# FFN way down by seven half-size products in three of four parts, and hidden columns mixed as they are made

## The chip, the cores and the metric

One core of one Trainium2 chip runs the whole program: two layers of a decoder trunk for one sequence of 512 tokens, 1024 wide, all in float32. The metric is the time of one execution on the device in microseconds (us). The engines are PE (TensorE, matrix products), DVE (VectorE), ACT (ScalarE), POOL (GpSimd) and SP (SyncE, which issues most of the loads).

## The reference, cut to what matters

Each layer is an FFN, a mix of attention and pooling, and a second FFN; so there are four FFNs, of 1024 by 2816.

```
def swiglu(h, w_gate, w_up, w_down):
    return (jax.nn.silu(h @ w_gate) * (h @ w_up)) @ w_down
...
for l in range(DEPTH):
    h = rms_norm(x, ffn1_norm[l])
    x = x + 0.5 * swiglu(h, ffn1_w_gate[l], ffn1_w_up[l], ffn1_w_down[l])
    ...
    h = rms_norm(x, ffn2_norm[l])
    x = x + 0.5 * swiglu(h, ffn2_w_gate[l], ffn2_w_up[l], ffn2_w_down[l])
return rms_norm(x, final_norm)
```

## The kernel before, in words

x is kept transposed in SBUF: eight blocks of 128 channels, each with 512 columns (the tokens). Every factor of a product is split into a rounded hi part and a lo part that holds the rest, and `mm3` (L95 to L97) makes each product of three matmuls: hi by hi, hi by lo, lo by hi.

The 2816 hidden channels of an FFN are 22 blocks of 128, taken as 11 pairs. For a pair, `plain` makes gate and up the direct way, with matmuls of 128x512 (one pair in each FFN, two in the first one); for the others, `mixed` makes them by Winograd's form of Strassen's method. Gate and up are there the two block rows of a matrix and the two halves of the tokens the two block columns, so that seven products take the place of eight. Each of them is 24 matmuls of 128x256 and needs mixed operands (the b's, made by `operands` at the start of an FFN) and mixed weights. Products are numbered by their operand, and are made in the order 1, 2, 6, 5, 7, 3, 4, in three PSUM banks (`ps_a`, `ps_g`, `ps_c`); some results are copied out by ACT (p1, w, p5 in `copied`, L451) and added by DVE. The pair's hidden columns, silu(gate) times up, are split by `hidden` into hhi and hlo.

The FFN runs in three parts, `PARTS`, of 4, 4 and 3 pairs. Behind each part's gate and up comes its way down: for each of the eight output blocks n, `down` makes 2 x nq products of 128x512 (three matmuls each) in a bank `ps_dn` and takes half of the sum off x (L499; the sign is turned in the hidden columns).

Weights come through two rings. `load_raw` has SP load blocks of up to 128x1024 into one of six raw buffers (wraw). `load_next` then makes the hi and lo part in one of five buffers each (whi, wlo). Most blocks are split by ACT and DVE (`split`, L143 and L144). A block by DMA goes another way: ACT writes the negative rounded value into wlo (L164), POOL issues a DMA that adds the block from HBM to it (L165, 512 KB each), and ACT casts the hi part (L166). For a mixed pair, `pair` plans seven blocks: products 1, 2 and 4 take theirs from memory as they are, by such a DMA; those of products 6, 5, 7 and 3 are sums of the four raw blocks, made on DVE (L175 to L178) and split there. `weights` hands out the next block and prepares the ones to come.

The order on each engine is the framework's scheduler's; a stretch marked `high_priority` may be moved ahead of others. Each engine then works through its own queue in order.

Of the kernel before, what the change touches and what calls it, by code (L numbers as in the profile page):

```python
# [11 lines left out]
F32 = mybir.dt.float32  # L12
# [9 lines left out]
L = 2  # L22
# [9 lines left out]
PARTS = ((0, 4), (4, 4), (8, 3))  # L32
# [38 lines left out]
def trunk(ctx: ExitStack, tc: tile.TileContext, xT, gu1, dn1, win_qk, win_v, win_u, poolw, wout, gu2, dn2, small, lams, consts, outT):  # L71
# [4 lines left out]
    act = ctx.enter_context(tc.tile_pool(name="act", bufs=25))  # L76
    tmp = ctx.enter_context(tc.tile_pool(name="tmp", bufs=8))
# [75 lines left out]
    def load_next(i):  # L153
# [15 lines left out]
        else:  # L169
            if step[0] == "sums":  # L170
                r = step[1] - 3
                load_raw(r + 3 + AHEAD_RAW)
                a11, a12, a21, a22 = raw_tiles[r : r + 4]
                u1 = wpool.tile([P, WSLOT], F32, name="wsum", bufs=1)
# [8 lines left out]
            split(hi, lo, raw)  # L183
# [22 lines left out]
    cst = cpool.tile([P, K_MASK], F32, name="cst")  # L206
# [130 lines left out]
    def triples(out, w, b, jj, start, stop, more):  # L337

        for i in range(4):
            c = slice((jj * 4 + i) * P, (jj * 4 + i + 1) * P)  # L340
            mm3(out, w[0][:, c], w[1][:, c], b[0][:, i, :], b[1][:, i, :], start and i == 0, stop and i == 3, more)

    def operands(norm, r):
# [13 lines left out]
        def parts(t):  # L357
            hi, lo = quarter("bhi", F32R), quarter("blo", F32R)
            split(hi, lo, t)
            return hi, lo  # L360
# [23 lines left out]
    def ffn(norm, l, nxt, first=None):  # L384
        st = {}
        hh, hl = [], []

        def hidden(u):

            hi, lo = arena("hhi"), arena("hlo")  # L390
            split(hi, lo, u)
            hh.append(hi)
            hl.append(lo)

        def plain(first, at):

            banks = [bank("ps_pl") for _ in range(4)]
            gates, u = [], pair32("u")
# [30 lines left out]
            for jj in range(2):  # L429
                v = u[:, jj, :]  # L430
                nc.vector.scalar_tensor_tensor(v, banks[2 + jj], -1.0, st["r"], ALU.mult, ALU.mult)
                nc.vector.tensor_mul(v, v, gates[jj])
            hidden(u)

        def halves(t):
            return t.rearrange("p (j s) -> p j s", j=2)

        def mixed():

            b = st["b"]  # L440
            u = pair32("u")

            def product(q, ps, start):
                w = weights()
                for jj in range(2):
                    triples(ps[:, jj * HS : (jj + 1) * HS], w, b[q], jj, start and jj == 0, True, True)

            def copied(ps, name):
                t = single(name)
                with tc.high_priority(PRIO):  # L450
                    nc.scalar.copy(t, ps)  # L451
                return t

            a, g, c = bank("ps_a"), bank("ps_g"), bank("ps_c")
            product(1, a, True)
            p1 = copied(a, "p1")
            product(2, g, True)
# [4 lines left out]
            product(6, a, False)  # L462
            w = copied(a, "w")
            product(5, c, True)
            p5 = copied(c, "p5")
            product(7, a, False)
            up2 = single("up2")
            with tc.high_priority(PRIO):
                nc.vector.tensor_add(up2, a, p5)
            product(3, c, False)  # L470
# [4 lines left out]
            product(4, a, False)  # L475
            with tc.high_priority(PRIO):
                nc.vector.tensor_mul(u[:, :, :HS], halves(a), halves(g1))
            nc.vector.tensor_mul(u[:, :, HS:], halves(up2), halves(g2))
            hidden(u)

        for hf, (q0, nq) in enumerate(PARTS):
            hh.clear()
            hl.clear()
            for q in range(q0, q0 + nq):
                if q >= plain_pairs(first):
                    mixed()
                elif q:
                    plain(None, -2)
# [12 lines left out]
            tail = hf == len(PARTS) - 1  # L501
            last = tail and isinstance(nxt, Final)
            if first and hf == 0:
                constants()
            for n in range(KD - 2 if last else KD):
                down(bank("ps_dn"), n, weights())
                if tail:
                    nxt.add(n)
# [17 lines left out]
    def mix(norm, l, nxt):  # L526
        st = {}

        def qk_project(h):
# [12 lines left out]
            if h == 0:  # L542
# [5 lines left out]
                st["cos"], st["sin"] = single("cosr"), single("sinr")  # L548
                nc.gpsimd.tensor_mul(st["cos"], cst[:, K_COS : K_COS + S], r)
                nc.gpsimd.tensor_mul(st["sin"], cst[:, K_SIN : K_SIN + S], r)  # L550
# [120 lines left out]
        def u_project(pair):  # L671
            dh, dl = arena("dhi"), arena("dlo")

            def done(i, ps):
# [15 lines left out]
                nc.vector.tensor_mul(e[:, :w], cur[:, :w], cst[:, K_CNT : K_CNT + w])  # L690
# [99 lines left out]
    def first_project(ps):  # L790
# [4 lines left out]
        for b in (A11, A12):  # L795
            raw.append(wpool.tile([P, 2, 4, P], F32, tag="wraw", name="wraw", bufs=6))
# [20 lines left out]
    def constants():  # L817
        nc.sync.dma_start(lam, lams)
        nc.sync.dma_start(cst, consts[:, :K_MASK])
# [120 lines left out]
```

## Time and profile before

| | us |
|---|---|
| median of 3 runs (1766.63 to 1768.07) | 1768.03 |
| the profiled execution | 1764.0 |
| its span | 1762.2 |
| PE busy (98% of the span) | 1728.4 |
| PE weight loads busy (89%) | 1565.5 |
| DVE busy (65%) | 1137.4 |
| ACT busy (54%) | 946.4 |
| POOL busy (12%) | 208.7 |

The span goes from the first to the last instruction; the execution's own time has 1.8 us more around it. Busy times overlap, since the engines run beside one another. A matmul's duration in a row is longer than its share of PE's time, because matmuls are pipelined: the time of one is read from how many start in a stretch. The granted clock, 0.995 in the mean, is the share of full speed that TensorE was given.

### The profile page before, as it was taken

The page shows a single profiled execution, that of the slowest core. Times are in us where ns is not written, and L with a number is a line of the kernel's source. Part 1 is how long each engine was busy: PE and PEld are TensorE (multiplying, and loading weights), DVE is VectorE, ACT ScalarE, POOL GpSimd, SP SyncE. Part 2 cuts the span into 40 slices and gives each one's busy share as a digit, 9 for nine tenths or more (in the row PEclk, how much of TensorE's full clock was granted, in tenths as well). Part 3 has the DMA queues.
Part 4 walks back from the last instruction along what each step waited for, and adds up shares of the span by engine and source line. Part 5 has one row for each costly group of instructions (what it writes and reads, how often), then busy time and mean ns, then how long its engine had stood idle before and what let it go on. Part 6 is the DMA issues. An engine that isn't in the chain of part 4 may idle for free.

```text
span 1762.2 us, 26872 instructions
## 1 busy us (share of the span) xinstructions
PE 1728.4 (98%) x10936; PEld 1565.5 (89%) x10936; DVE 1137.4 (65%) x1507; ACT 946.4 (54%) x1294; POOL 208.7 (12%) x215
## 2 busy tenths in 40 slices
PE   9899999999999999999999999999999999999997
PEld 7889989888788989989889899898887889899996
DVE  6845646577968746646587465466789596466463
ACT  7635626555566626526556265364555665364463
POOL 1000001120022001001210010012100400010001
PEclk9999999999999999999999999999999999999998
DMA  9455746422235737737657376374122647375551
GB/s 285 121 155 147 190 116 158 143 86 75 72 92 134 197 106 168 192 87 169 181 124 195 84 182 185 96 169 147 42 86 68 151 105 201 95 185 165 118 146 48
DMA packets 71723, 240.66 MB, mean 137 GB/s; under 512 B 7856, under 2 KB 12592, under 8 KB 71600
## 3 DMA queue, kind: packets, MB, share of 16 engines
q1 hardware_dynamic: 52304, 169.18, 30.3%
q0 software_dynamic: 19152, 69.74, 21.9%
q8 instruction: 85, 1.39, 0.3%
q14 instruction: 38, 0.31, 0.0%
q10 hardware_dynamic: 144, 0.03, 0.0%
HBM read 236.82 MB, written 2.10 MB: 136 GB/s over the span
## 4 chain that ended last, share of the span: by engine, by line
PE 87%; DVE 4%; DMA 4%; issue 2%; ACT 2%; SPq 0%; POOL 0%; POOLq 0%; DVEq 0%; ACTq 0%
PE ps_dn L96 9%; PE ps_dn L95 9%; PE ps_dn L97 9%; PE ps_a L97 8%; PE ps_a L96 8%; PE ps_a L95 8%; PE ps_c L95 4%; PE ps_c L96 4%; PE ps_c L97 4%; DMA wlo<-gu 3%; PE ps_g L97 2%; PE ps_g L95 2%; PE ps_g L96 2%; PE ps_pl L97 2%; PE ps_pl L95 2%
## 5 line engine op out<-in xcount | busy, mean ns | idle before, releaser
L143 ACT CAST whi<-wraw 128x1024 fp32r<-128x1024 f32 (+2 forms) x275 | 273.7, 997 | 417.1 <-PE ps_dn L96 146.3
L144 DVE TENSOR_TENSOR wlo<-wraw,whi 128x1024 fp32r<-128x1024 f32 (+2 forms) x275 | 317.6, 1157 | 109.3 <-ACT whi L143 107.6
L97 PE MATMUL ps_a<-bhi,wlo 128*128 128x256 f32 x1248 | 354.7, 284 | 4.9 <-DMA wlo<-gu 4.9
L95 PE MATMUL ps_a<-bhi,whi 128*128 128x256 f32 x1248 | 354.6, 284 | 0.8 <-ACT whi L166 0.5
L96 PE MATMUL ps_a<-blo,whi 128*128 128x256 f32 x1248 | 354.6, 284 | 0.0
L96 PE MATMUL ps_dn<-hlo,whi 128*128 128x512 f32 (+1 forms) x716 | 276.6, 386 | 0.0
L97 PE MATMUL ps_dn<-hhi,wlo 128*128 128x512 f32 (+1 forms) x716 | 276.0, 386 | 0.0
L95 PE MATMUL ps_dn<-hhi,whi 128*128 128x512 f32 (+1 forms) x716 | 275.7, 386 | 0.0
L165 POOL DMA_DIRECT2D wlo<-gu x133 | 116.3, 877 | 1117.7 <-ACT wlo L164 846.3
L97 PEld LDWEIGHTS ps_a<-bhi,wlo 128*128 128x128 f32 x1248 | 240.7, 193 | 5.6 <-DMA wlo<-gu 5.6
L95 PEld LDWEIGHTS ps_a<-bhi,whi 128*128 128x128 f32 x1248 | 240.6, 193 | 1.9 <-ACT whi L166 0.7
L96 PEld LDWEIGHTS ps_a<-blo,whi 128*128 128x128 f32 x1248 | 240.7, 193 | 0.8
L166 ACT CAST whi<-wraw 128x1024 fp32r<-128x1024 f32 x133 | 139.3, 1049 | 135.2 <-PE ps_dn L96 62.2
L499 DVE SCALAR_TENSOR_TENSOR x<-ps_dn,x 128x512 f32<-128x512 f32 (+1 forms) x98 | 66.6, 680 | 192.2 <-PE ps_dn L97 192.2
L95 PE MATMUL ps_c<-bhi,whi 128*128 128x256 f32 x624 | 177.0, 284 | 5.7 <-ACT bhi L143 5.7
L96 PE MATMUL ps_c<-blo,whi 128*128 128x256 f32 x624 | 176.8, 283 | 0.0
L97 PE MATMUL ps_c<-bhi,wlo 128*128 128x256 f32 x624 | 176.7, 283 | 0.0
L96 PEld LDWEIGHTS ps_dn<-hlo,whi 128*128 128x128 f32 x716 | 134.5, 188 | 28.0 <-DVE hlo L144 1.4
L97 PEld LDWEIGHTS ps_dn<-hhi,wlo 128*128 128x128 f32 x716 | 134.5, 188 | 26.9
L95 PEld LDWEIGHTS ps_dn<-hhi,whi 128*128 128x128 f32 x716 | 134.5, 188 | 26.7
L164 ACT ACTIVATE wlo<-wraw 128x1024 fp32r<-128x1024 f32 x133 | 140.3, 1057 | 0.2 <-DMA wraw<-gu 0.2
L95 PEld LDWEIGHTS ps_c<-bhi,whi 128*128 128x128 f32 x624 | 119.9, 192 | 6.3 <-ACT bhi L143 6.3
(171 smaller groups left out, 3231.8 us busy)
## 6 DMA issues: line engine op xcount, KB each, us to landing
wraw<-gu SPq DMA_DIRECT2D x174, 512.0 KB, 3.7
wlo<-gu POOLq DMA_DIRECT2D x133, 512.0 KB, 7.1
wraw<-dn SPq DMA_DIRECT2D x64, 512.0 KB, 4.5
wraw<-dn SPq DMA_DIRECT2D x32, 384.0 KB, 3.1
wraw<-wqk SPq DMA_DIRECT2D x16, 512.0 KB, 3.5
wraw<-wo SPq DMA_DIRECT2D x16, 512.0 KB, 3.6
wraw<-wv SPq DMA_DIRECT2D x8, 512.0 KB, 3.5
wraw<-wu SPq DMA_DIRECT2D x8, 512.0 KB, 3.6
```

The source lines that it names most:

```text
L95: nc.tensor.matmul(out, a_hi, b_hi, start=start, stop=False, skip_group_check=more)
L96: nc.tensor.matmul(out, a_hi, b_lo, start=False, stop=False, skip_group_check=more)
L97: nc.tensor.matmul(out, a_lo, b_hi, start=False, stop=stop, skip_group_check=more)
L143: nc.scalar.copy(hi, raw)
L144: nc.vector.tensor_sub(lo, raw, hi.bitcast(F32))
L164: nc.scalar.mul(lo[:, :n], raw[:, :n], -1.0)
L165: nc.gpsimd.dma_start(lo[:, :n], src, accum_op=ALU.add)
L166: nc.scalar.copy(hi[:, :n], raw[:, :n])
L499: nc.vector.scalar_tensor_tensor(x[:, n, ts], ps[:, ts], -0.5, x[:, n, ts], ALU.mult, ALU.add)
```

## The change

The way down of three parts is now made by seven half-size products as well. `PARTS` becomes 3, 3, 3 and 2 pairs; only the last part keeps `down`. For a part of nq pairs, `mixed_down` makes the eight output blocks as two halves (n = 0, 1) of four; in each half the two pairs of output blocks, the two blocks of each hidden pair and the two halves of the tokens are the blocks of the method. A product there is 6 x nq = 18 matmuls of 128x256, in the banks `ps_da`, `ps_dg` and `ps_dc`, and two to four updates of x on DVE (L531, L534) belong to it in place of one per output block. In the first half, products 1 and 2 are written so that what needs the newest hidden pair comes behind what doesn't.

`hidden` also makes the four mixed columns that these products need (ehi, elo, L432 to L438). A plain pair's last steps (up by gate, and `hidden`) are put off: they are a `finish` that the next mixed pair calls behind its fourth product. The down weights of these parts are planned by `pair`, three of seven blocks by DMA (384 KB each). The ring of raw weights has five buffers in place of six, the two pools act and tmp one more each. The table of cosines and sines is loaded for each mix instead of kept.

```
-PARTS = ((0, 4), (4, 4), (8, 3))
+PARTS = ((0, 3), (3, 3), (6, 3), (9, 2))
...
-                for n in range(KD):
-                    block(dn[hf][l, n])
+                if hf < len(PARTS) - 1:
+                    for n in range(2):
+                        pair(dn[hf][l, n])
+                else:
+                    for n in range(KD):
+                        block(dn[hf][l, n])
...
-            raw = wpool.tile([P, WSLOT], F32, name="wraw", bufs=6)
+            raw = wpool.tile([P, WSLOT], F32, name="wraw", bufs=5)
...
+        def hidden(first, second):
             hi, lo = arena("hhi"), arena("hlo")
-            split(hi, lo, u)
+            hs, ls = slots(hi), slots(lo)
+            if st["mixed"]:
+                split(hs[:, 3, :], ls[:, 3, :], second[:, 1, :])
+            else:
+                split(hs[:, 1::2, :], ls[:, 1::2, :], second)
+            split(hs[:, 0::2, :], ls[:, 0::2, :], first)
...
+            nc.vector.tensor_sub(e5, first[:, 0, :], second[:, 0, :])
+            nc.vector.tensor_sub(e7, second[:, 1, :], second[:, 0, :])
+            split(es[:, 0:2, :], fs[:, 0:2, :], halves(e))
...
+            nc.vector.scalar_tensor_tensor(e6, e5, -1.0, second[:, 1, :], ALU.mult, ALU.subtract)
+            nc.vector.scalar_tensor_tensor(e4, e6, -1.0, first[:, 1, :], ALU.mult, ALU.subtract)
+            split(es[:, 2:4, :], fs[:, 2:4, :], halves(e))
...
             p5 = copied(c, "p5")
+            if "finish" in st:
+                st.pop("finish")()
...
+        def mixed_down(n, nq):
...
+            if n == 0:
+                w1, w2 = weights(), weights()
+                product(a, w1, b[1], True, False, range(nq - 1))
+                product(g, w2, b[2], True, False, range(nq - 1))
+                product(a, w1, b[1], False, True, range(nq - 1, nq))
+                p1 = copied(a, "p1", -0.5)
+                product(g, w2, b[2], False, True, range(nq - 1, nq))
+            else:
+                product(a, weights(), b[1], True)
+                p1 = copied(a, "p1", -0.5)
+                product(g, weights(), b[2], True)
+            add(x1[:, :, first], g, -0.5)
+            plus(x1[:, :, first], p1)
+            product(a, weights(), b[6], False)
+            w = copied(a, "w", -0.5)
+            product(c, weights(), b[5], True)
+            p5 = copied(c, "p5", 0.5)
+            product(a, weights(), b[7], False)
+            with tc.high_priority(PRIO):
+                add(x2[:, :, second], a, 0.5)
+            plus(x2[:, :, second], p5)
+            product(c, weights(), b[3], False)
+            add(x1[:, :, second], c, -0.5)
+            plus(x1[:, :, second], w)
+            product(a, weights(), b[4], False)
+            add(x2[:, :, first], a, 0.5)
...
-            for n in range(KD):
-                down(bank("ps_dn"), n, weights())
+            if not tail:
+                for n in range(2):
+                    mixed_down(n, nq)
+                continue
```

What moves on the engines is seen at three places. The first is ACT's queue in the first FFN's way down. Before, at its first part, the queue holds casts of whole blocks behind the last hidden columns:

```order
L143 CAST whi<-wraw 128x1024
L143 CAST hhi<-u 128x1024
L143 CAST whi<-wraw 128x1024 x3
L166 CAST whi<-wraw 128x1024
L164 ACTIVATE wlo<-wraw 128x1024
L166 CAST whi<-wraw 128x1024
L164 ACTIVATE wlo<-wraw 128x1024
L143 CAST whi<-wraw 128x1024
```

After, at its second part, from product 1's copy in the first half on (blocks of 128x768 are the way down's, p and w the copies out of PSUM, L358):

```order
L358 ACTIVATE p_2044<-ps_da 128x512
L147 CAST ehi<-e_1998 128x512
L168 ACTIVATE wlo<-wraw 128x768
L170 CAST whi<-wraw 128x768 x2
L358 ACTIVATE w<-ps_da 128x512
L358 ACTIVATE p_2104<-ps_dc 128x512
L168 ACTIVATE wlo<-wraw 128x768 x2
```

And in the second half of the same part:

```order
L358 ACTIVATE p_2214<-ps_da 128x512
L170 CAST whi<-wraw 128x768
L168 ACTIVATE wlo<-wraw 128x768
L170 CAST whi<-wraw 128x1024
L358 ACTIVATE w<-ps_da 128x512
L168 ACTIVATE wlo<-wraw 128x1024
```

The negative copies (L168) for the second half's first two products now stand behind the copies of the third and fourth product (w and p_2104); those of the next gate and up pair (128x1024) stand in the second half in the same way.

The second place is POOL's queue in the same FFN. Before, its DMAs are all for gate and up:

```order
L165 DMA wlo<-gu 128x1024 x2
L298 TENSOR_TENSOR rT<-ms,nhalf 128x4
L165 DMA wlo<-gu 128x1024 x29
L251 TENSOR_TENSOR ssum<-ssum,sq 128x512 x7
```

After:

```order
L169 DMA wlo<-gu 128x1024 x2
L304 TENSOR_TENSOR rT<-ms,nhalf 128x4
L169 DMA wlo<-gu 128x1024 x5
L169 DMA wlo<-dn 128x768 x6
L169 DMA wlo<-gu 128x1024 x9
L169 DMA wlo<-dn 128x768 x6
L169 DMA wlo<-gu 128x1024 x9
L169 DMA wlo<-dn 128x768 x6
L169 DMA wlo<-gu 128x1024 x6
L257 TENSOR_TENSOR ssum<-ssum,sq 128x512 x7
```

Six DMAs for down weights now stand between those for gate and up, three times in each FFN.

The third place is PE's queue in the first mixed pair of the second FFN, at the end of its sixth product. Before (bhi_5366 is the operand of product 4):

```order
L96 MATMUL ps_c_5399<-blo_5363,whi_5430 128x256
L97 MATMUL ps_c_5399<-bhi_5362,wlo_5431 128x256
L95 MATMUL ps_a_5397<-bhi_5366,whi_5461 128x256
L96 MATMUL ps_a_5397<-blo_5367,whi_5461 128x256
L97 MATMUL ps_a_5397<-bhi_5366,wlo_5462 128x256
```

After (bhi_6007 is the operand of product 1, and ps_a_6351 the next pair's bank):

```order
L96 MATMUL ps_c_6076<-blo_6049,whi_6107 128x256
L97 MATMUL ps_c_6076<-bhi_6048,wlo_6108 128x256
L95 MATMUL ps_a_6351<-bhi_6007,whi_6169 128x256
L96 MATMUL ps_a_6351<-blo_6008,whi_6169 128x256
L97 MATMUL ps_a_6351<-bhi_6007,wlo_6170 128x256
```

The next pair's first product stands here ahead of this pair's last, product 4.

## Rows read from the trace of the kernel before

**Rows 1.** The page: busy time of each engine, shares of the chain of waits.

```profile
PE 1728.4 (98%) x10936; PEld 1565.5 (89%) x10936; DVE 1137.4 (65%) x1507; ACT 946.4 (54%) x1294; POOL 208.7 (12%) x215
...
PE 87%; DVE 4%; DMA 4%; issue 2%; ACT 2%; SPq 0%; POOL 0%; POOLq 0%; DVEq 0%; ACTq 0%
```

**Rows 2.** Windows by stage, first FFN: first gate/up stretch, way down, second gate/up stretch.

```profile
core 0: us, PE busy (x) PEld busy (x) DVE busy (x) ACT busy (x) POOL busy (x), PEclk, DMA share, GB/s
53.00:100.00 47.00, 42.49 (x337) 41.90 (x336) 34.98 (x40) 27.52 (x33) 3.50 (x4) 0.96 0.61 164
100.00:143.56 43.56, 43.56 (x194) 36.07 (x193) 18.91 (x21) 11.29 (x11) 1.75 (x2) 1.00 0.40 102
143.56:224.19 80.63, 80.63 (x673) 80.63 (x672) 52.39 (x53) 52.10 (x61) 8.75 (x10) 1.00 0.71 183
```

**Rows 3.** PE's waits over the span: total us, times, longest.

```profile
PE ps_c L95 <- ACT bhi L143: 5.7, 3, 1.9
...
PE ps_a L97 <- DMA wlo<-gu: 4.9, 3, 4.0
```

**Rows 4.** Timelines of PE, ACT and POOL, 192.3 to 204.4: start us, duration us.

```profile
192.39 0.28 PE L97 MATMUL ps_a<-bhi,wlo 128*128 128x256 f32 x1
...
192.64 1.05 ACT L166 CAST whi<-wraw 128x1024 fp32r<-128x1024 f32 x1 [0.19 <-PE ps_a L96]
193.59 0.58 ACT L451 COPY w<-ps_a 128x512 f32<-128x512 f32 x1
194.07 1.06 ACT L164 ACTIVATE wlo<-wraw 128x1024 fp32r<-128x1024 f32 x1
...
195.42 0.88 POOL L165 DMA_DIRECT2D wlo<-gu  x1 [2.49 <-ACT wlo L164]
...
204.27 0.28 PE L97 MATMUL ps_a<-bhi,wlo 128*128 128x256 f32 x1
```

**Rows 5.** Landings, stretches 100:143, 143:213, 275:285; then those issued 155.10, 175.26, 195.42.

```profile
DMA to landing us min/median/max: 5.3/5.4/5.6
...
DMA to landing us min/median/max: 5.8/7.0/7.6
...
DMA to landing us min/median/max: 7.9/8.2/8.2
...
DMA to landing us min/median/max: 6.8/6.8/6.8
...
DMA to landing us min/median/max: 6.2/6.2/6.2
...
DMA to landing us min/median/max: 7.1/7.1/7.1
```

**Rows 6.** Groups of instructions, shapes apart, whole span: busy us, mean ns, idle before.

```profile
L144 DVE TENSOR_TENSOR wlo<-wraw,whi 128x1024 fp32r<-128x1024 f32 x231 | 281.9, 1223 | 89.0 <-ACT whi L143 88.3
...
L143 ACT CAST whi<-wraw 128x768 fp32r<-128x768 f32 x32 | 26.7, 836 | 52.4 <-issue 23.4 <-PE ps_dn L96 13.6 <-PE ps_c L96 8.2
```

**Rows 7.** The page's DMA issues: count, size, median us from issue to landing.

```profile
wraw<-dn SPq DMA_DIRECT2D x64, 512.0 KB, 4.5
wraw<-dn SPq DMA_DIRECT2D x32, 384.0 KB, 3.1
```

**Rows 8.** Second FFN, first mixed pairs: timeline of POOL and PE, landing of that DMA.

```profile
569.52 0.86 POOL L165 DMA_DIRECT2D wlo<-gu  x1 [2.66 <-PE ps_c L97]
...
DMA to landing us min/median/max: 7.0/7.0/7.0
...
575.24 0.28 PE L97 MATMUL ps_a<-bhi,wlo 128*128 128x256 f32 x1
```

**Rows 9.** Windows behind the starts of three FFNs (columns as in rows 2).

```profile
66.00:88.00 22.00, 18.04 (x138) 17.83 (x137) 15.21 (x16) 13.25 (x16) 2.62 (x3) 0.92 0.75 187
...
562.00:584.00 22.00, 20.68 (x171) 20.57 (x171) 21.79 (x24) 17.68 (x22) 2.57 (x3) 1.00 0.62 142
...
1422.00:1444.00 22.00, 20.11 (x152) 19.70 (x151) 20.40 (x24) 15.75 (x18) 2.60 (x3) 0.92 0.55 130
```

More of the change, by code (lines that the diff above doesn't have):

```diff
@@ L172, in load_next @@
                 load_raw(r + 3 + AHEAD_RAW)
-                a11, a12, a21, a22 = raw_tiles[r : r + 4]
-                u1 = wpool.tile([P, WSLOT], F32, name="wsum", bufs=1)
+                n = raws[r].shape[-1]
+                a11, a12, a21, a22 = (raw[:, :n] for raw in raw_tiles[r : r + 4])
+                u1 = wpool.tile([P, WSLOT], F32, name="wsum", bufs=1)[:, :n]
                 nc.vector.tensor_add(u1, a21, a22)
@@ L182, in load_next @@
                 raw = sums[step[2]][step[1]]
-            split(hi, lo, raw)
+            n = raw.shape[-1]
+            split(hi[:, :n], lo[:, :n], raw)
         loaded.append((hi, lo))
@@ L335, in run, with product, copied, halves @@
             pass
[L337 to L341, printed above, removed]
+    def product(ps, w, b, start, stop=True, ks=None):
+        ks = ks or range(len(b))
+        for jj in range(2):
+            out = ps[:, jj * HS : (jj + 1) * HS]
+            for i in ks:
+                c = slice((jj * len(b) + i) * P, (jj * len(b) + i + 1) * P)
+                mm3(out, w[0][:, c], w[1][:, c], *b[i], start and jj == 0 and i == ks[0], stop and i == ks[-1], True)
+    def copied(ps, name, scale=None):
+        t = single(name)
+        with tc.high_priority(PRIO):
+            if scale is None:
+                nc.scalar.copy(t, ps)
+            else:
+                nc.scalar.mul(t, ps, scale)
+        return t
+    def halves(t):
+        return t.rearrange("p (j s) -> p j s", j=2)
+    def slots(t):
+        return t.rearrange("p j (h s) -> p (j h) s", h=2)
     def operands(norm, r):
@@ L359, in parts @@
             split(hi, lo, t)
-            return hi, lo
+            return [(hi[:, i, :], lo[:, i, :]) for i in range(4)]
         b = {}
@@ L428, in plain, with finish @@
                 gated()
[L429 to L436, printed above, removed]
+            def finish():
+                u = single("u1"), single("u2")
+                for jj in range(2):
+                    v = single("up")
+                    nc.vector.scalar_tensor_tensor(v, banks[2 + jj], -1.0, st["r"], ALU.mult, ALU.mult)
+                    for half in range(2):
+                        ts = slice(half * HS, (half + 1) * HS)
+                        nc.vector.tensor_mul(halves(u[half])[:, jj, :], v[:, ts], gates[jj][:, ts])
+                hidden(halves(u[0]), halves(u[1]))
+            st["finish"] = finish
         def mixed():
             b = st["b"]
[L441 to L452, printed above, removed]
             a, g, c = bank("ps_a"), bank("ps_g"), bank("ps_c")
-            product(1, a, True)
+            product(a, weights(), b[1], True)
             p1 = copied(a, "p1")
-            product(2, g, True)
+            product(g, weights(), b[2], True)
             g1 = single("g1")
@@ L483, in ffn @@
             hl.clear()
+            hb[:] = [{} for _ in range(nq)]
+            tail = hf == len(PARTS) - 1
+            st["mixed"] = not tail
             for q in range(q0, q0 + nq):
@@ L795, in first_project @@
         for b in (A11, A12):
[L796 removed]
+            raw.append(wpool.tile([P, 2, 4, P], F32, tag="wraw", name="wraw", bufs=5))
             hi.append(wpool.tile([P, 2, 4, P], F32R, tag="whi", name="whi", bufs=5))
@@ L891, in down @@
         w = cols(w)
-        return [w[:, :, :, 2 * q0 : 2 * (q0 + nq), :].reshape(L, KD, P, 2 * nq * P) for q0, nq in PARTS]
+        parts = [w[:, :, :, 2 * q0 : 2 * (q0 + nq), :] for q0, nq in PARTS]
+        mixed = [p.reshape(L, 2, 2, 2, P, nq, 2, P).transpose(0, 1, 2, 6, 4, 3, 5, 7).reshape(L, 2, 4, P, 2 * nq * P) for p, (_, nq) in zip(parts[:-1], PARTS)]
+        return mixed + [parts[-1].reshape(L, KD, P, -1)]
     def blocks(gate, up):
```

73 lines of the change are left out of this document (49 added, 24 removed).

## The prediction

> **What bounds the kernel now.** I read five views in this order. The page first: TensorE (PE) is busy 98% of a span of 1762.2 us and carries 87% of the chain of waits [rows 1], so time can only come out of PE's own stream, or be lost where PE is made to wait. Second, the windows by stage: in the stretch of half-size products (143.56 to 224.19) PE and its weight loads are both busy for the whole 80.63 us; in a stretch of the FFN's way down (100.00 to 143.56) PE is still full, its weight loads are not, and VectorE (DVE), ScalarE (ACT) and the DMA engines are about half as busy as before it [rows 2]. The way down is now the stage in which the other engines catch up. Third, the list of PE's waits: the whole span has only three or four that matter to an FFN, 5.7 us on a split operand and 4.9 us on an accumulating DMA [rows 3]. Fourth, the timeline of one weight block that is split by such a DMA, from the freed buffer to the landing [rows 4]. Fifth, the landings of these DMAs in stretches of different traffic [rows 5].
>
> **What PE gains.** By rows 2 the half-size stretch holds 4 pairs of 7 products of 24 matmuls, 672 in 80.63 us: 0.1200 us a matmul of 256 columns. The way-down stretch holds 8 outputs of 24 matmuls, 192 in 43.56 us: 0.2269 us a matmul of 512 columns. For a pair of hidden blocks the way down costs 8 x 2 x 3 = 48 wide matmuls now (10.89 us) and 2 x 7 x 6 = 84 narrow ones after (10.08 us). Nine of eleven pairs change in each of four FFNs: 36 x 0.81 = **29.0 us** less. So 12.5% fewer columns give only 7.4%, because a narrow matmul takes over half of a wide one: 0.1200 against 0.1134. The Trainium skill (TensorE: Matmul & The Clock Gate, "Back-to-back issue gap") gives N/2.4 + 2.5 ns for an isolated matmul, 109 ns and 216 ns here, and says that beside weight loads the spacing is set by both. By its isolated figures the gain would be an estimated 42.7 us; by rows 2 the weight loads fill the narrow stretch wall to wall, so the trace decides for 29.0.
>
> **What it adds off PE.** Mixing the hidden columns (two subtractions and two combined ones of 256 columns, two more splits), the weight sums, and two updates of x per product in place of one per output all go to DVE and ACT in a stage where DVE was busy 18.9 of 43.56 us and ACT 11.3 [rows 2]. DVE was busy 52.4 of 80.63 us, 65%, beside the same kind of weights in the narrow stage, so I cost this work at nothing, covered by PE's products, except at places where PE waits for one result. Walking the queues through with the durations of rows 6, DVE comes to some 80% in a pair. If that cover fails, the price is as in the first part of the first FFN (below).
>
> *Seam from gate/up to way down.* The program puts the parts of the first two products that need only the earlier pairs (24 matmuls, 2.9 us) ahead of those that need the newest. The last mixed block ends some 6.7 us after the last gate/up product, behind eight DVE instructions (splits of up to 1.22 us [rows 6]); the scheduler has laid the products so that it is first read then. I take **0.1 us**.
>
> *First product of the second half of outputs* (a 384 KB block split by DMA). Five buffers for weights make its hi part wait for the third product of the first half. That ends at 67 x 0.12 = 8.04 us, the cast of 0.84 [rows 6] makes 9.0, PE would read at 8.74: 0.3 us. Behind the cast on ACT stands the copy of the third product's result (0.48 a step [rows 4]), for which the next product waits: another 0.25. Then its lo part: on ACT the sign-turned copy is queued behind the copy of the fourth product, so that it ends near 10.7, the DMA goes out 0.3 later, at 11.0. No 384 KB accumulating DMA is in the trace. From above, it takes as long as one of 512 KB, 7.0 at the median [rows 5]; from below, as a plain 384 KB load, 3.1 [rows 7]. I scale 7.0 by the plain loads, 3.1 to 4.5 [rows 7]: 4.8. It lands at 15.8; PE asks for it at 15.4 plus the 0.55 already lost, so it is just in time. **0.57 us** (0.57 also with 3.1, 2.6 with 7.0).
>
> *First product of the next gate/up pair.* In the narrow stage the chain reads: the old buffer's last matmul at 192.39, cast 192.64, copy 193.59, sign-turned copy 194.07, DMA 195.42, landed 7.1 later at 202.52, read at 204.27 [rows 4, 5]. That is 2.9 us from release to issue, and 1.75 us to spare out of 11.88. After the change the buffer is freed by the third product of the second half, and four shorter products stand between: 4 x 2.16 + 0.24 = 8.88 us. So PE waits for all that the landing takes over 8.88 - 2.90 = **5.98 us**. The three loads in this place in the narrow stage took 6.8, 6.2 and 7.1 [rows 5]; the down stretch had 5.3 to 5.6, but with DMA engines 40% busy, where the new one moves as many bytes per us as the narrow stage (71%). I take 6.8: **0.8 us** (0 with 5.4, 2.2 with 8.2).
>
> Twelve parts change (three in each FFN): 12 x 1.47 = 17.6 us.
>
> *Starts of FFN 2 to 4.* The scheduler now puts the second pair's first product ahead of the first pair's last. Its lo block was issued at 569.52 and took 7.0 [rows 8], landing at 576.5; the third matmul in that place came at 575.24 [rows 8]: 1.3 us. The blocks behind it I put at 0.5. Three times 1.8, less the 0.9 us of such waits that are there already ([rows 3]: 4.9, of which 4.0 is the first FFN's): **4.5 us** (0 to 8). The wait of 1.9 us on a split operand [rows 3] stays. *First FFN, first part:* 336 matmuls (40.3 us) take 47.00 now [rows 2], 6.7 lost; the walk gives 7.9 for it after, **1.2** more. *Last parts* (two pairs, plain): **1.0** for POOL, which adds up squares there and also issues the DMAs.
>
> SP's queue loses nothing: a raw buffer fewer (five for six), but a part's loads of 384 KB are shorter. The constants now read anew for each mix stand ahead of its first use by tens of us.
>
> **Sum.** -29.0 + 17.6 + 4.5 + 1.2 + 1.0 = -4.7 us. The profiled execution took 1764.0 us, which gives 1759.3; the median of the runs, 1768.03, lies 4.0 higher, which gives **1763.3**, 0.27% less. A change under 0.2% (3.5 us) can't be told from none.
>
> **Rivals.**
> 1. *The landings are in time.* If the new stage leaves DMAs as short as in the old way down, 5.3 to 5.6 [rows 5], the gate/up wait is gone (0.67 a part, 8.0) and the FFN starts cost 0.6: -29.0 + 8.0 + 0.6 + 2.2 = -18.2, **1749.8**. For it: the loads of the way down are a quarter shorter. Against it: the same bytes per us as the narrow stage.
> 2. *The landings are late* (slower). One mechanism, in the two places of each part: the accumulating DMA is the longest link between a freed buffer and the product. It decides from a landing of 5.98 us on; the worst in a narrow stage were 7.9 to 8.2 [rows 5]. At 8.2 the two waits are 1.3 and 2.2, a part 3.6, twelve 43.4, the FFN starts, each 1.2 more, 3 x 3.0 - 0.9 = 8.1: -29.0 + 43.4 + 8.1 + 2.2 = +24.7, **1792.7**. For it: raw loads, accumulating DMAs and their issues no longer get a quiet stretch. The Trainium skill (SBUF — State Buffer, "SBUF: two separate sides") warns that DMAs issued by GpSimd can starve while DVE holds the port that they share, which would put a busier DVE on this side. The trace fits, but can't tell that from traffic: with DVE 65% and DMA 71% busy the median is 7.0, with 43% and 40% it is 5.4 [rows 2, 5].
> 3. *Waits bring the clock down* (slower). After the 4.0 us wait of the first FFN (66 to 88), and after one of the 1.9 us waits (1422 to 1444), the granted clock shows 0.92 over 22 us; after another (562 to 584) it stays at 1.00 [rows 3, 9]. Each dip costs 22 x 0.08 = 1.8 us. Against it: the new waits are shorter. If the new waits, 15 places, cause one at half of them: +13 on the sum, **1776**.
> 4. *The narrow products of the way down don't run at 0.12.* They are the same form, so little speaks for it: it needs weight loads that cover better or worse in groups of 18 than of 24. At 0.1134 (half a wide one) the gain grows by 36 x 84 x 0.0066 = 20, to 1743; as much the other way gives 1783.
>
> **Chances.** As summed 0.45, its own range 1755 to 1773; rival 1 0.24, rival 2 0.16, rival 3 0.11, rival 4 0.04. The summed case lies half below the 0.2% line (0.23 faster, 0.12 same, 0.10 slower): faster 0.23 + 0.24 + 0.02 = 0.49, same 0.12, slower 0.10 + 0.16 + 0.11 + 0.02 = 0.39. The range that keeps 8 in 10 goes from rival 1 to short of rival 2's upper half: **1747 to 1790**.
>
> **What would show it.** PE's stream: 0.12 us for every matmul of the new way down, and 29 us less busy time without waits. In the list of PE's waits, two new groups of some 12 each: the way down's first product on the hi cast and the copy (0.2 to 0.3 each), gate/up's first product on the accumulating DMA (0.8). The landing of the 384 KB DMA should be near 4.8 and that of the 512 KB one near 6.8. Wrong would be: waits at the seam on the split of the mixed columns, PE waiting for DVE anywhere in a steady pair, or landings that differ by over 1 us from these.

## The result and the profile after

The changed kernel takes 1810.62 us in the median of 4 runs (1805.47 to 1815.27), against 1767.33 us for the kernel before on the same chip: a ratio of 1.0242 with a 95% interval of 1.0226 to 1.0258. It is slower by 43 us, where 4.7 us less was forecast; the time lies outside the range of 1747 to 1790. The profiled execution took 1809.65 us, its span is 1807.9 us against 1762.2, so the two traces differ by 45.7 us.

The page of the changed kernel (span; busy times; the chain of waits):

```profile
span 1807.9 us, 30756 instructions
...
PE 1733.0 (96%) x12220; PEld 1616.7 (89%) x12220; DVE 1381.2 (76%) x2009; ACT 1128.6 (62%) x1658; POOL 269.4 (15%) x287
...
PE 67%; DMA 12%; DVE 8%; issue 8%; ACT 4%; POOL 1%; SPq 1%; POOLq 0%; DVEq 0%; ACTq 0%
...
wlo<-gu POOLq DMA_DIRECT2D x133, 512.0 KB, 7.4
wraw<-dn SPq DMA_DIRECT2D x96, 384.0 KB, 3.2
wlo<-dn POOLq DMA_DIRECT2D x72, 384.0 KB, 6.8
```

PE's share of the chain fell from 87% to 67% [rows 1]; DMA, DVE and waiting to issue took its place. The new accumulating DMAs of 384 KB land after 6.8 us in the median, hardly sooner than those of 512 KB.

The windows by stage, first FFN (the first stretch holds all of the first part, then come gate/up, way down, gate/up), which answer to [rows 2]:

```profile
core 0: us, PE busy (x) PEld busy (x) DVE busy (x) ACT busy (x) POOL busy (x), PEclk, DMA share, GB/s
52.74:124.52 71.78, 58.74 (x421) 55.97 (x420) 58.88 (x85) 41.21 (x59) 7.88 (x9) 0.88 0.56 132
124.52:185.12 60.60, 60.60 (x506) 60.53 (x505) 46.37 (x59) 40.79 (x54) 7.85 (x9) 1.00 0.73 178
185.12:216.94 31.82, 31.51 (x255) 30.51 (x253) 25.89 (x35) 21.71 (x30) 5.26 (x6) 1.00 0.76 179
216.94:278.62 61.68, 60.73 (x506) 60.52 (x505) 47.10 (x60) 40.79 (x54) 7.85 (x9) 1.00 0.72 178
```

504 matmuls at 0.12 us are 60.48 us, so the gate/up stretch at 124.52 runs as before. A half-size way down is 252 of them, 30.24 us: it took 31.82, and the stretch behind it 1.2 us more than its matmuls. The first stretch has 420 matmuls, 50.4 us, and took 71.78.

PE's longest sums of waits (total us, times, longest), which answer to [rows 3]:

```profile
PE ps_da L97 <- DMA wlo<-dn: 8.6, 12, 1.5
PE ps_c L95 <- ACT whi L147: 6.4, 1, 6.4
PE ps_da L95 <- ACT whi L170: 5.8, 15, 0.8
PE ps_s L700 <- DVE qs L659: 5.7, 6, 1.2
PE ps_c L95 <- ACT bhi L147: 5.5, 3, 1.9
PE ps_r L315 <- DVE rb L312: 5.1, 3, 2.4
PE ps_a L97 <- DMA wlo<-gu: 4.4, 6, 1.3
PE ps_pl L96 <- DVE xlo L247: 4.2, 3, 2.2
```

The two groups that were looked for are there (on the DMAs wlo, and on the cast at L170). Others were not expected: rb and xlo, the norm at the start of an FFN, of which the kernel before has only one wait of 1.4 us on rb, at its very end; and one wait of 6.4 us on a cast, in the first FFN.

Taken stage by stage, a stage's excess being its time less its matmuls at 0.1200 and 0.2269 us, the 45.7 us come out so:

| stage | forecast | measured |
|---|---|---|
| fewer columns, same pitch (3000 narrow matmuls more, 1716 wide ones fewer) | -29.0 | -29.4 |
| first FFN, first part (excess 21.4 for 6.7) | +1.2 | +14.7 |
| starts of FFN 2 to 4, plain stretches (26.9, 28.8, 27.3 us for 23.2 each) | 0 | +13.5 |
| the same, gate/up behind them (7.0 each for 2.7, 3.2, 4.5) | +4.5 | +10.6 |
| ways down and gate/up behind them (11 here; forecast for 12) | +17.6 | +31.9 |
| the two mixes (173.5, 172.8 us for 171.1 each) | 0 | +4.1 |
| last parts | +1.0 | +0.4 |

Part of what is lost at the starts is the clock. The mean granted clock fell from 0.995 to 0.987: by (1 - clock) x span, as if PE had been busy throughout, about 9 us were lost before and about 23 now. The plain stretches of FFN 2 to 4 show it:

```profile
548.00:574.94 26.94, 25.29 (x109) 20.28 (x108) 18.74 (x28) 12.30 (x14) 4.26 (x4) 0.94 0.50 114
904.62:933.45 28.83, 25.29 (x109) 20.29 (x108) 18.99 (x28) 12.14 (x15) 5.83 (x6) 0.94 0.58 138
1436.00:1463.33 27.33, 25.09 (x109) 20.43 (x108) 18.76 (x28) 12.28 (x14) 4.32 (x4) 0.94 0.50 113
```

What PE waits for there is on DVE's timeline, here at the start of the third FFN (PE starts it at 904.62):

```profile
905.23 0.69 DVE L586 SCALAR_TENSOR_TENSOR x<-ps_dn,x 128x512 f32<-128x512 f32 x1
911.74 1.23 DVE L180 TENSOR_TENSOR wsum<-wraw 128x1024 f32<-128x1024 f32 x1 [5.82 <-DMA wraw<-gu]
913.00 1.22 DVE L181 TENSOR_TENSOR wraw<-wraw 128x1024 f32<-128x1024 f32 x1
914.14 0.74 DVE L247 SCALAR_TENSOR_TENSOR xlo<-x,sm,xhi 128x512 fp32r<-128x512 f32 x1
914.80 1.22 DVE L182 TENSOR_TENSOR wraw<-wraw,wsum 128x1024 f32<-128x1024 f32 x1
915.94 0.15 DVE L302 TENSOR_SCALAR ms<-ps_ms 128x4 f32<-128x4 f32 x1
917.24 0.43 DVE L312 COPY rb<-rT 128x512 f32<-128x512 f32 x1 [1.15 <-POOL rT L304]
```

DVE stands idle for 5.8 us at the head of its queue: the first weight sum of the FFN's first mixed pair waits for a raw block. Behind it stand the norm's last split (xlo) and its sums (ms, rb). In the kernel before the same sum began 6.1 us ahead of PE's start of that FFN, at 873.61 for 879.69; now it begins 7.1 us behind it.

```profile
873.61 1.23 DVE L175 TENSOR_TENSOR wsum<-wraw 128x1024 f32<-128x1024 f32 x1 [1.19 <-DMA wraw<-gu]
```

The raw block it needs was issued at 869.5 before, 10.2 us ahead of PE's start, and at 903.0 now, 1.6 ahead (both read from SP's issues). It took 4.0 and 8.7 us to land. So the sum is late by about 8.6 us of issue and 4.7 of landing.

### The profile page after: what moved, and what is told of

The parts are those of the page before. It is cut to its first block, busy times and chain, and to the rows that moved or that the text cites. A ratio compares the mean times of both kernels' runs of the same rounds, so it can differ in the third digit from the quotient of the medians.

```text
span 1807.9 us, 30756 instructions
## 1 busy us (share of the span) xinstructions
PE 1733.0 (96%) x12220; PEld 1616.7 (89%) x12220; DVE 1381.2 (76%) x2009; ACT 1128.6 (62%) x1658; POOL 269.4 (15%) x287
## 4 chain that ended last, share of the span: by engine, by line
PE 67%; DMA 12%; DVE 8%; issue 8%; ACT 4%; POOL 1%; SPq 1%; POOLq 0%; DVEq 0%; ACTq 0%
PE ps_a L97 8%; PE ps_a L96 8%; PE ps_a L95 8%; DMA wlo<-dn 7%; PE ps_c L95 4%; PE ps_c L97 4%; PE ps_c L96 4%; DMA wlo<-gu 3%; DMA wraw<-gu 2%; PE ps_g L97 2%; PE ps_g L95 2%; PE ps_g L96 2%; PE ps_da L95 2%; PE ps_pr L95 1%; DVE wlo L148 1%
## 5 line engine op out<-in xcount | busy, mean ns | idle before, releaser
L147 ACT CAST whi<-wraw 128x1024 fp32r<-128x1024 f32 (+3 forms) x283 | 259.4, 919 | 256.3 <-PE ps_a L96 97.7
L148 DVE TENSOR_TENSOR wlo<-wraw,whi 128x1024 fp32r<-128x1024 f32 (+3 forms) x283 | 301.7, 1069 | 44.0 <-ACT whi L147 42.0
L170 ACT CAST whi<-wraw 128x1024 fp32r<-128x1024 f32 (+1 forms) x205 | 198.6, 970 | 108.9 <-issue 60.0
L168 ACT ACTIVATE wlo<-wraw 128x1024 fp32r<-128x1024 f32 (+1 forms) x205 | 199.5, 981 | 0.2 <-DMA wraw<-gu 0.2
L180 DVE TENSOR_TENSOR wsum<-wraw 128x1024 f32<-128x1024 f32 (+1 forms) x63 | 70.8, 1124 | 115.9 <-DMA wraw<-gu 91.7
L97 PE MATMUL ps_da<-ehi,wlo 128*128 128x256 f32 x432 | 123.2, 285 | 5.2 <-DMA wlo<-dn 5.2
L95 PE MATMUL ps_da<-ehi,whi 128*128 128x256 f32 x432 | 125.7, 291 | 0.6
L97 PEld LDWEIGHTS ps_c<-bhi,wlo 128*128 128x128 f32 x624 | 120.3, 193 | 3.5 <-DVE wlo L148 3.5
L96 PE MATMUL ps_da<-elo,whi 128*128 128x256 f32 x432 | 122.5, 284 | 0.0
L96 PEld LDWEIGHTS ps_c<-blo,whi 128*128 128x128 f32 x624 | 120.4, 193 | 0.0
```

The lines of the kernel that those rows point to most:

```text
L95: nc.tensor.matmul(out, a_hi, b_hi, start=start, stop=False, skip_group_check=more)
L96: nc.tensor.matmul(out, a_hi, b_lo, start=False, stop=False, skip_group_check=more)
L97: nc.tensor.matmul(out, a_lo, b_hi, start=False, stop=stop, skip_group_check=more)
L147: nc.scalar.copy(hi, raw)
L148: nc.vector.tensor_sub(lo, raw, hi.bitcast(F32))
L168: nc.scalar.mul(lo[:, :n], raw[:, :n], -1.0)
```

## The experiments

Three theories. **A**: five raw buffers in place of six make the raw blocks late, and DVE's queue holds the norm up behind them. **B**: the mixed columns and the half-size way down of an FFN's first part come where DVE is full already. **C**: the accumulating DMAs are too long for products this short. Each run's ratio is to the kernel before on the same chip. Stages named below are excess over the matmuls, worked out as in the table.

**A raw buffer fewer, in the kernel before**

```
-            raw = wpool.tile([P, WSLOT], F32, name="wraw", bufs=6)
+            raw = wpool.tile([P, WSLOT], F32, name="wraw", bufs=5)
```

> The kernel before with five raw weight buffers in place of six, nothing else. Theory A (the missing raw buffer makes the first weight sum of an FFN late, and DVE's queue holds the norm up behind it): slower by 10 to 18 us, with PE waits on xlo or rb and clock dips at the starts of FFN 2 to 4. Theory B (the mixed columns of the first part are what hurts) and theory C (late landings of the added DMAs): within 3 us of before.

Measured: 1791.79 us against 1767.48, 1.0126 (1.0101 to 1.0152). The windows of its second FFN (plain stretch, the gate/up stretch behind it, and the three stretches that follow):

```profile
544.31:571.70 27.39, 25.06 (x109) 20.36 (x108) 18.75 (x28) 12.29 (x14) 4.33 (x4) 0.94 0.51 117
571.70:638.67 66.97, 62.89 (x505) 62.16 (x504) 50.97 (x56) 43.33 (x51) 6.02 (x7) 0.97 0.65 165
638.67:806.40 167.73, 167.73 (x1058) 152.73 (x1057) 90.56 (x92) 74.43 (x83) 12.09 (x14) 1.00 0.55 139
```

and the same of the kernel before:

```profile
532.21:555.40 23.19, 23.19 (x109) 19.31 (x108) 15.90 (x25) 12.18 (x14) 5.30 (x5) 1.00 0.60 132
555.40:618.57 63.17, 61.16 (x505) 60.64 (x504) 51.62 (x56) 43.60 (x51) 6.03 (x7) 1.00 0.68 175
618.57:786.30 167.73, 167.73 (x1058) 152.73 (x1057) 90.02 (x92) 74.72 (x83) 12.11 (x14) 1.00 0.55 139
```

The buffer costs 24 us by itself, more than theory A asked for, and nearly all of it at the starts. Its profiled execution, its longest run, has a span 32.4 us longer than before, of which 10.2 are in the first FFN's first gate/up stretch, 12.0 in the three plain stretches and 9.0 in the gate/up stretches behind them. In the middle of an FFN it costs nothing: the same three stretches take 167.73 us with five and with six.

**First part's way down plain**

```
-                if hf < len(PARTS) - 1:
+                if 0 < hf < len(PARTS) - 1:
...
-            st["mixed"] = not tail
+            st["mixed"] = hf > 0 and not tail
```

> The changed kernel with the first part's way down plain again in every FFN (its columns unmixed); the two middle parts stay by half-size products. It gives up 9.7 us of the products' gain. Theory B: the 14.7 us lost in the first FFN's first part and about 10 us at the other starts go, with four parts' waits (11 us): 1810 - 36 + 10 = about 1784. Theory A: the plain stretches at the starts keep their 13.5 us and the first part wins little: 1800 or more. Theory C: a third of the DMA waits go, 1810 + 10 - 5 = 1815.

Measured: 1788.85 us, 1.0124 (1.0109 to 1.0139), 22 us faster than the changed kernel although 9.7 us of the products' gain are given up. Both theories take part: the gate/up stretches at the starts of FFN 2 to 4 came back to 4.5, 3.7 and 4.9 (before 2.7, 3.2, 4.5), as B said, while the plain stretches kept 4.3, 5.2 and 7.0 for 1.4 before, as A said. The first FFN's first gate/up stretch is whole again, though there are still five raw buffers:

```profile
52.85:80.07 27.22, 22.33 (x170) 21.68 (x168) 24.01 (x33) 15.28 (x21) 0.87 (x1) 0.94 0.45 133
```

It has 168 matmuls, 20.16 us, so it loses 7.1, for 6.7 before and 21.4 in the changed kernel.

**Product 1's block without a DMA**

```
-        plan.append(("block", r, True))
+        plan.append(("block", r, False))
```

> The changed kernel with product 1's weight block of every mixed pair and every half-size way down split by ACT and DVE instead of the accumulating DMA. Theory C: most of PE's 14.2 us of waits on those DMAs go and clock dips with them if they cause any: about 1798. Theories A and B: DVE has more to do at the starts, nothing gained there; 1805 to 1815. If DVE becomes the bound in steady pairs, slower than 1815.

Measured: 1798.78 us, 1.0178 (1.0157 to 1.02), as theory C had it. The waits of gate/up on product 1 are gone (stretches behind a way down at 60.48 us, no excess). What is left is the wait on the way down's other DMAs. PE waits more than in the changed kernel on weights split by DVE (5.9 us for 2.6), and the plain stretches of FFN 2 to 4 lose 26.2 us for 17.8, so DVE's extra work at the starts, which A and B had expected, came too:

```profile
PE ps_c L97 <- DVE wlo L148: 5.9, 4, 1.5
...
PE ps_da L97 <- DMA wlo<-dn: 4.8, 8, 1.6
```

**Last steps of a plain pair at once**

```
-            st["finish"] = finish
+            finish()
```

> The changed kernel with a plain pair's last steps done at once instead of behind the next mixed pair's fourth product. Theory B in the form that the order of these steps is at fault: the first FFN's start improves by 5 to 10 us, 1800 to 1805. Theories A and C: within 4 us of 1810, or slower, since DVE does the same work earlier.

Measured: 1842.11 us, 1.0426 (1.0401 to 1.0452): 31 us worse. The deferral is the part of the change that helps; without it the gate/up stretches at the starts of FFN 2 to 4 have 15 to 17 us of excess for 7.0. In the changed kernel DVE is busy 43.5 of the 47.5 us there (574.94 to 622.48) and ACT 32.9, so DVE is nearly full, as B says; that the order was at fault is not so.

**The first weight sum pinned**

```
-                nc.vector.tensor_add(u1, a21, a22)
+                ins = nc.vector.tensor_add(u1, a21, a22)
+                if i > 8 and plan[i - 4][0] == "block" and plan[i - 6][0] == "block" and raws[r - 4].shape == raws[r].shape:
+                    in_order(ins)
```

> The changed kernel with one DVE instruction pinned behind what was traced before it: the first weight sum of each FFN's first mixed pair. Its raw blocks still come late (five buffers), but the norm no longer stands behind it in DVE's queue. Theory A: the plain stretches at the starts of FFN 2 to 4 lose most of their 13.5 us of excess, waits and clock dips: 1798 to 1802; the gate/up stretches behind them stay as late as they were, or later. If the late sum itself (not the queue) is what counts: no change, 1810.

Measured: 1799.71 us, 1.018 (1.0164 to 1.0195). The plain stretches are whole again:

```profile
541.88:565.07 23.19, 23.19 (x109) 19.30 (x108) 16.99 (x26) 12.19 (x14) 4.12 (x4) 1.00 0.56 127
897.17:920.38 23.21, 23.21 (x110) 19.30 (x108) 17.56 (x27) 12.41 (x15) 5.91 (x6) 1.00 0.73 176
```

(`in_order` keeps an instruction behind those that were written before it on its engine.) So the queue behind the late sum is what holds the norm up. But the late sum is still to come, and the gate/up stretches behind now have 9 to 11 us of excess for 7.0: of the 13.5 us that the plain stretches had lost, 8.9 come back later. The first FFN's first part, whose first sum is pinned as well, has 15.5 us of excess for 21.4.

**All three remedies**

It is the kernel with the first part plain, with the edits for product 1 and for the pin on top.

> First part plain, product 1 of every mixed pair split without a DMA, and the first weight sum pinned: 1789 - 8 (DMA waits of eight parts) - 10 (plain stretches) = about 1770. If the three remedies share one cause (say the clock dips), less than their sum: 1778.

Measured: 1776.18 us, 1.0047 (1.0032 to 1.0062): less than the sum of the three, and near the 1778 given for that case. The gate/up stretches at the starts lose 7 to 10 us each (before 2.7 to 4.5), as behind the pin alone, and the two mixes 6.9 in all.

**Shorter half-size parts, six raw buffers**

```
-PARTS = ((0, 3), (3, 3), (6, 3), (9, 2))
+PARTS = ((0, 4), (4, 2), (6, 2), (8, 3))
...
-    act = ctx.enter_context(tc.tile_pool(name="act", bufs=26))
+    act = ctx.enter_context(tc.tile_pool(name="act", bufs=24))
...
-            raw = wpool.tile([P, WSLOT], F32, name="wraw", bufs=5)
+            raw = wpool.tile([P, WSLOT], F32, name="wraw", bufs=6)
```

> Six raw buffers again, made room for by parts of 4, 2, 2 and 3 pairs of which the two middle ones alone go by half-size products (product 1 split without a DMA). The products' gain is 4 x 4 x 0.81 = 12.9 us. Theory A: the FFN starts are as in the kernel before, and what is lost is only in the eight short half-size ways down, some 1.5 us each: 1763 to 1770. If the starts stay late with six buffers, theory A is wrong: 1785 or more. If DVE is full in the shorter ways down (products of 1.44 us): 1775 to 1785.

Measured: 1820.13 us, 1.0296 (1.0266 to 1.0327), none of the three cases as stated. The plain stretches are whole (23.18, 23.21 and 23.19 us), as A said; the gate/up stretches behind them are not (8.1, 6.8 and 6.5 us of excess, for 2.7, 3.2 and 4.5 before), and why is open. Most is lost in the ways down of two pairs, whose products last 1.44 us for 2.16: 5.5 to 8.0 us each (27.56 us for 20.16 in the first). Its waits, and its row of DMA issues:

```profile
PE ps_da L97 <- DMA wlo<-dn: 28.6, 16, 2.5
PE ps_a L97 <- DMA wlo<-gu: 12.6, 8, 2.7
```

```profile
wlo<-dn POOLq DMA_DIRECT2D x32, 256.0 KB, 6.0
```

That speaks for theory C: a block of half the size lands after 6.0 us in the median, and four products between a freed buffer and its use are 5.8 us. But DVE is busy 24.4 us of those 27.56, so the case of a full DVE isn't ruled out as a part of it.

**The parts alone, in the kernel before**

```
-PARTS = ((0, 4), (4, 4), (8, 3))
+PARTS = ((0, 3), (3, 3), (6, 3), (9, 2))
```

> The kernel before with parts of 3, 3, 3 and 2 pairs, nothing else. All theories: the same time within 3 us, 1765 to 1770; more would mean that one part more costs something by itself.

Measured: 1775.86 us against 1767.62, 1.0046 (1.0029 to 1.0063): 8.2 us that no theory had. 5.4 us of it are the third FFN's plain stretch (28.60 us for 23.20), which comes right behind a last part of two pairs; 3.1 are in the mixes. In that stretch DVE waits at the first weight sum as in the changed kernel, though there are six raw buffers:

```profile
886.97 1.23 DVE L175 TENSOR_TENSOR wsum<-wraw 128x1024 f32<-128x1024 f32 x1 [4.36 <-DMA wraw<-gu]
```

So at the third FFN two parts of the change make the raw block late, and each takes about half of the lead:

| kernel, start of the third FFN | block issued ahead of PE's start | landing | sum begins |
|---|---|---|---|
| before | 10.2 us | 4.0 us | 6.1 us ahead |
| five raw buffers | 6.1 | 6.9 | 0.9 behind |
| new parts | 5.8 | 8.5 | 2.8 behind |
| both (the changed kernel) | 1.6 | 8.7 | 7.1 behind |

With the new parts alone the plain stretches of the second and fourth FFN, which come behind a mix, take 23.2 us as before.

**Six raw buffers beside half-size ways down**

With the first part plain its pairs can be finished as in the kernel before, and eight scratch buffers do for nine, which makes room for a sixth raw buffer. Product 1 goes without a DMA in the half-size ways down and right behind them. The two kernels differ in these two lines, and in a third that repeats the count of raw buffers where the first blocks are loaded:

```
-    tmp = ctx.enter_context(tc.tile_pool(name="tmp", bufs=9))
+    tmp = ctx.enter_context(tc.tile_pool(name="tmp", bufs=8))
...
-            raw = wpool.tile([P, WSLOT], F32, name="wraw", bufs=5)
+            raw = wpool.tile([P, WSLOT], F32, name="wraw", bufs=6)
```

> First part plain as in the kernel before (pairs finished at once, columns unmixed); product 1 split without a DMA in the half-size ways down and in the gate/up pair right behind one; five raw buffers, no pin. Control for the next kernel. Theory A: the starts stay late, 1775 to 1785.

Measured: 1784.75 us, 1.0109 (1.0093 to 1.0124).

> The same with six raw buffers (and one scratch buffer fewer, eight, to make room). Theory A: 10 to 20 us faster than the one with five, the plain stretches at 1.4 us of excess. By the sum: 1767.5 - 19.3 (six pairs in four FFNs) + 10.4 (eight half-size ways down at 1.3) + 8.2 (what parts of 3, 3, 3 and 2 cost the kernel before) = 1767. If the raw ring isn't the cause, no faster than the control.

Measured: 1772.24 us, 1.0034 (1.0022 to 1.0047): the sixth buffer is worth 12.5 us here. The first FFN's first part has 6.9 us of excess for 15.8, and two of three plain stretches are at 1.4 us; the third FFN's has 7.8 (8.1 with five), much as in the kernel with the parts alone (6.8).

**Parts of 2, 3, 3 and 3 pairs**

```
-PARTS = ((0, 3), (3, 3), (6, 3), (9, 2))
+PARTS = ((0, 2), (2, 3), (5, 3), (8, 3))
```

> The same with six raw buffers and parts of 2, 3, 3 and 3 pairs, so that the last way down keeps three pairs as in the kernel before; the two parts of three in the middle go by half-size products. If the cost of the parts of 3, 3, 3 and 2 came from the shorter last part: 1759 to 1763, faster than the kernel before. If the shorter first way down gives the loads too little time at the start of an FFN: 1767 to 1775.

Measured: 1761.45 us against 1766.13, 0.9971 (0.996 to 0.9983), faster than the kernel before. The third FFN's plain stretch has 2.4 us of excess for 7.8.

**And product 4's block without a DMA**

```
-        plan.append(("block", r + 3, True))
+        plan.append(("block", r + 3, gu.shape[-1] == WSLOT))
```

> The kernel with parts of 2, 3, 3 and 3 pairs and six raw buffers, with product 4's block of the half-size ways down split by ACT and DVE too, so that in those only product 2 has a DMA. In the kernel without this, PE waits 5.7 us in all (7 times, 1.5 at most) for the DMA of product 4 in the first half of outputs. Theory C (an accumulating DMA is too long for these short products): those waits go, 3 to 6 us faster, about 1757 against 1766 of before. If DVE is full there: new waits on split weights, 1761 or more.

Measured: 1756.8 us against 1766.54, 0.9932 (0.9916 to 0.9947). Every half-size way down now has 1.05 or 1.07 us of excess, and PE's only wait on an accumulating DMA is one of 0.2 us; DVE, busy 1338.4 us, holds:

```profile
PE 1719.6 (98%) x11800; PEld 1597.0 (91%) x11800; DVE 1338.4 (76%) x1906; ACT 1042.7 (59%) x1517; POOL 216.6 (12%) x223
...
wlo<-dn POOLq DMA_DIRECT2D x16, 384.0 KB, 4.6
```

So the idea pays 0.7% (0.5 to 0.8) where it is kept to two parts in four and its loads are in time.

## Why the prediction was wrong

**PE's gain** held: the narrow stretches run at 0.12 us a matmul (504 in 60.48), and the sum has 29.4 us for the 29.0 (36 x 0.81 is 29.2). The isolated spacing of the Trainium skill (TensorE: Matmul & The Clock Gate, "Back-to-back issue gap"), 109 and 216 ns, doesn't fit these streams, which run at 120 and 227. The page keeps it for a single matmul and says that in a stream of weight loads and matmuls both set the spacing.

**Work off PE** held in the steady stages: DVE is busy 77% of the gate/up stretch at 124.52 and 81% of the way down behind it, for the forecast 80%, and no wait on DVE is in them. (The updates of x are 168 of 128x512, one per product; the prediction counted two.) At the starts the cover failed.

**The step that failed worst** is the shortest one: "SP's queue loses nothing: a raw buffer fewer (five for six), but a part's loads of 384 KB are shorter." A ring is not a matter of load times. The first weight sum of an FFN's first mixed pair needs the FFN's eighth block. With six buffers that block goes where the plain pair's second block was, with five where its third was, so its load can't be issued until one more block has been read: in the kernel before, SP's issues are 4.1 us apart there (865.4, 869.5, 873.6), and with five buffers the load goes out 4.1 us later. In the middle of an FFN that costs nothing; at a start it is 24 us in the kernel before, and 12.5 between two kernels with half-size ways down. The trace of before couldn't show the wait, but it showed the margin, which I didn't look up: the sum of the third FFN began 6.1 us ahead of PE's start, with the raw block landed 0.1 us earlier.

**The new parts** were priced at 1.0 us, for POOL. Alone, in the kernel before, they cost 8.2: behind a last part of two pairs the loads of the next FFN have 4.4 us less of a lead. That is the same wait as the buffer's, and at the third FFN the two add up.

**Starts of FFN 2 to 4**: 24.1 us for 4.5. The waits that I had placed in the gate/up stretch were there in kind. In the second FFN they were 0.9 on the cast for the way down's first product, 0.7 on a copy and 0.4 on a split weight, and only 0.2 on the DMA that I priced at 1.3. With the first part plain these stretches are nearly as before, so their 10.6 us are mostly the price of that part's half-size way down. What was missing was the 13.5 us of the plain stretch, which the buffer and the parts cause, and the clock: the starts of FFN 2 to 4 have a dip of about 1.7 us in each plain and in each gate/up stretch, for one in all before.

**First FFN**: 14.7 for 1.2. PE waited 6.4 us for ACT's casts of weight sums; the second sum stood on DVE behind the mixing of the first pairs' columns, and DVE was busy without a break from 53 to 65 us. The kernel with the first part plain tells the causes apart: with five raw buffers still, it loses 7.1 there, 0.4 more than before. So here it is the first part's mixed columns and half-size way down. The missing buffer costs 9 to 10 us in this place only in kernels that finish a plain pair at once (10.2 in the kernel before, 8.9 between the two kernels that differ in it).

**Twelve ways down**: 31.9 us for 17.6. The mechanism was right, and so was the place for the hi cast (0.25 us in each part) and the copy. The term that was mis-sized is the landing of the 384 KB DMA: scaled from plain loads to 4.8 us, measured 6.8. The scaling itself was good: in the last kernel, with one such DMA in each half, the median is 4.6. What it left out is the traffic of the changed kernel, where none of the 72 is by itself. The upper bound, "as long as one of 512 KB", was the better guess there. I also placed its wait on the second half's product 1 alone; in the runs the second half's products 2 and 4 wait too, and product 4 in the first half (1.5 us at most), which the last experiment took away. The landing of 6.8 that I took for 512 KB blocks came out at 7.4. By the prediction's own signs, a landing off by over 1 us was one of being wrong, and so was a wait at the seam: the first FFN has one of 1.7 us there, on hlo.

**The rivals.** What came is rival 2 and rival 3 together, on top of causes that I had priced at next to nothing. Rival 2 had 1792.7 for late landings: leaving one of the three DMAs of each half in the last kernel's ways down ended those waits. Rival 3 had 13 us of clock dips: it was about 15, though not at most of the ways down, where the waits are short, but at the starts. The Trainium skill (SBUF — State Buffer, "SBUF: two separate sides") says that a DMA issued by GpSimd can wait for its descriptors while DVE holds the ports that they share. Where these runs can tell the two apart, it is traffic that goes with a long landing, and not a busier DVE (last section); no run changed DVE's work alone.

**The range** left out a price for the buffer that the change takes away: with its 24 us the sum itself would have stood near 1788, and with the 7 us that the parts cost beyond 1.0, near 1795, an estimate that takes the two to add up.

Open: the 4.1 us in the mixes. The kernel before with new parts shows 3.1 of them without the constants that are now loaded for each mix; but the last kernel, whose last part has three pairs again, still loses 4.9 there. The constants were not tried alone.

## What to carry to other kernels

Price a buffer that is taken out of a ring by the margin of the first consumer that needs the block (when it began, and when its block landed), never by the speed of the load; a late load at the head of an in-order queue holds up everything behind it, here the norm. Where a product gets shorter, count the products between a freed buffer and its next use against the whole chain that refills it: here 2.9 us to the issue and, in the changed kernel's traffic, some 7 us to the landing. And when a change is slower, try its parts apart before it is dropped: two of three half-size ways down, six raw buffers and plain splits gave 0.7% less than the kernel before.

## What the runs showed of the hardware that was not expected

In these runs an accumulating DMA's time goes with the traffic beside it more than with its size. The medians are 7.4 us for 512 KB and 6.8 for 384 KB in the changed kernel. In the kernel with short parts 256 KB took 3.7 to 4.1 us in the first half's product 2, and 7.0 to 8.0 in its product 4. In the last kernel the 384 KB DMAs of the second half, which go out with no other accumulating DMA under way, took 4.5 to 4.8. One of them, from issue to landing, and one of the kernel with parts of 2, 3, 3 and 3 pairs that still has product 4's DMA (first half, 8.7 us), columns as in the windows above:

```profile
243.54:248.24 4.70, 4.70 (x41) 4.70 (x41) 4.48 (x7) 2.10 (x3) 0.87 (x1) 1.00 0.50 87
...
240.19:248.89 8.70, 7.79 (x61) 7.18 (x59) 8.05 (x12) 5.37 (x8) 1.75 (x2) 1.00 0.89 209
```

DVE is as busy beside the short one (95%) as beside the long one (93%); the DMA engines are busy 50% and 89%, with plain loads and a second accumulating DMA in the long one's time. Plain loads took 3.2 us for 384 KB and 4.4 for 512 KB of gate and up, but 3.3 to 4.0 for 512 KB in the mixes.

Behind many of PE's waits of about 2 us at the starts of an FFN the granted clock stood at 0.66 over 5 us. In the changed kernel's fourth FFN it was so behind the wait of 2.2 us on xlo, and behind that of 1.9 on bhi:

```profile
1440.00:1445.00 5.00, 4.33 (x12) 3.50 (x13) 4.14 (x5) 1.24 (x2) 1.22 (x1) 0.66 0.93 193
1470.00:1475.00 5.00, 3.75 (x17) 3.65 (x18) 5.00 (x6) 4.56 (x6) 0.86 (x1) 0.66 0.10 16
```

A share of 0.66 is a part of the 5 us at 1.2 and the rest at 2.4 GHz; 1.7 us are lost, nearly as much as by the wait itself. In the kernel before, one of three waits of 1.9 us had such a dip behind it [rows 9] (the third FFN's stretch, 902.89 to 966.60, is at 1.00), now all three.
